# First column tiles in two halves of tokens, and the end of a hybrid encoder layer by column halves and tile by tile

## The chip, the cores and the metric

The kernel runs on one core of a Trainium2 chip. The metric is the device time of one execution in microseconds (us), the median of several runs. A core has five engines that run side by side, each through its own list of instructions in a fixed order: TensorE (PE in the profile, with its weight loads shown as PEld), VectorE (DVE), ScalarE (ACT), GpSimd (POOL) and SyncE (SP, which here only issues DMAs). An instruction waits on semaphores, and what stands behind it on its engine waits with it.

## The reference: what is computed

One encoder layer is applied to two batches with the same weights: P (prompt, 512 tokens) and S (sample, 1024 tokens), 1024 features, float32. Cut to what matters:

```python
u = group_rmsnorm(h, norm_mix_pre); proj = u @ w_in
# z, xbc, dt -> forward and backward chunked state-space scans (SSD head group)
# hy         -> width-3 conv, long convolution with implicit filters (Hyena head group)
mix = concat([y_ssd, y_hy]) @ w_out
h = h + group_rmsnorm(mix, norm_mix_post)
u = group_rmsnorm(h, norm_ffn_pre)
ff = (silu(u @ w_gate) * (u @ w_up)) @ w_down
h = h + group_rmsnorm(ff, norm_ffn_post)
gate = sigmoid(group_rmsnorm(h, ple_norm_pre) @ w_ple_gate)
e = p_l @ w_ple_proj
h = h + group_rmsnorm(gate * e, ple_norm_post)      # the last step of the layer
```

`group_rmsnorm(x, w)` is x divided by the root of the mean of its squares over the 1024 features, times the row `w`.

## The kernel before: tiling, stages and order

**Products.** A float32 operand is split into two `fp32r` parts, hi (a copy on ACT, lines 292 and 325) and lo (the rest, by a subtraction on POOL, line 293, for weights, and on DVE, line 326, for activations). `mm3` (lines 296 to 303) makes one product of three matmuls: hi by hi (L301), hi by lo (L302 or L303), lo by hi. Weights come by DMA into `wst` and are split into `whi` and `wlo`; each of the three has six buffers.

**Stages.** P: the input norm and its transposes (`make_u`, `norm_tile`, lines 328 to 370) give `uh` and `ul`, 1024 features by 512 tokens. `project` (line 431) then makes twelve tiles of 128 columns of `w_in`: `win_T` (line 375) multiplies eight feature blocks into one PSUM tile `g` of 512 tokens, 24 matmuls, and `conv` (line 384) reads it back on ACT and DVE. `gps` has two PSUM tiles, so the third column tile waits until the first has been read by `conv`. The weights of the first three tiles are loaded and split ahead (`pre`, line 1408). Then follow the filters of the long convolution (`filters`, lines 810 to 940), the scans, the long convolution, the same for S, the output projections, and the FFN of P. In the last stretch, for S, `down_group` makes the two groups of 512 tokens ready, and for each group `ple` (line 1374) and `ple_post` (line 1392) do the last two lines of the reference.

**The last group.** `ple` loads `e` into four tiles `ga` (128 tokens by 1024 columns) and calls `tok_gemm` (line 1007) with the gate weights. `tok_gemm` goes over two halves of 512 columns (`nch`), loads the eight feature blocks ("rows" below) of weights in four pairs, and multiplies each pair with four token tiles in the order 0, 2, 1, 3. With `last` set, it holds back the last two pairs of the second half (rows 4 to 7) and runs those tile by tile, so that tile 0 is complete first; 12 matmuls of each tile are then behind one another. After each half, `ev_gate` (line 1383) takes the sigmoid on ACT (L1386) and multiplies it into `ga` on DVE (L1387). `ple_post` calls `post_steps` (line 1040): the sum of squares of a whole row on ACT (L316), `rstd` (L308 on DVE, L309 on POOL), the gain row (L1056), the scaling and the residual (L1057) on DVE, and a DMA of 128 by 1024 to the output, issued by SP (L1061).

**What sets the order.** The program is written stage by stage, but the order of each engine's list is chosen when the program is built: line 1523 asks for a scheduler with a time line of its own estimates, and sections marked as urgent (`high_priority`) go first. So filters, scans and long convolutions are woven between the projection tiles, and a change near the start can alter the weave behind it.

Of the kernel before, what the change touches and what calls it, by code (L numbers as in the profile page):

```python
# [15 lines left out]
ALU = mybir.AluOpType  # L16
# [150 lines left out]
class Kern:  # L167
# [144 lines left out]
    def sumsq(self, pool, x):  # L312

        ss = self.T(self.sp, [128, 1], "ss")
        junk = self.T(pool, [128, x.shape[-1]], "junk", BF16, bufs=1)
        self.nc.scalar.activation(junk, x, AF.Square, accum_out=ss)  # L316
        return ss
# [57 lines left out]
    def win_T(self, q, u, c0, w=128, pre=None):  # L375
# [3 lines left out]
        for g in range(q.ng):  # L379
            for k in range(8):  # L380
                self.mm3(ps[:w, g, :], ws[k], u[g].row(k), k == 0, k == 7)
# [625 lines left out]
    def tok_gemm(self, lhs, nk, wsrc, krow0, evac, last=False, mid=None):  # L1007

        for nch in range(2):
# [7 lines left out]
            for k0 in range(0, nk, 2):  # L1017
# [5 lines left out]
                if last and nch == 1 and k0 + 4 >= nk:  # L1023
# [16 lines left out]
    def post_steps(self, pool, acc, row, res, t0, dst, gain=None, u=None, tags=("t4",) * 4, last=False):  # L1040
# [7 lines left out]
        def load(t):  # L1048
            rts[t] = self.T(pool, [128, 1024], tags[t])
            nc.sync.dma_start(rts[t], res[t0 + t * 128:t0 + (t + 1) * 128, :])  # L1050

        def add(t):
            a, r, rt = acc[t], rs[t], rts[t]
            if last:
                w = self.T(pool, [128, 1024], "t4")
                nc.vector.tensor_tensor(out=w, in0=a, in1=rw, op=ALU.mult)  # L1056
                nc.vector.scalar_tensor_tensor(rt, w, r, rt, ALU.mult, ALU.add)  # L1057
            else:
                nc.vector.scalar_tensor_tensor(a, a, r, rw, ALU.mult, ALU.mult)
                nc.vector.tensor_tensor(out=rt, in0=a, in1=rt, op=ALU.add)  # L1060
            (nc.sync if last else nc.gpsimd).dma_start(dst[t0 + t * 128:t0 + (t + 1) * 128, :], rt)  # L1061
# [38 lines left out]
    def outproj(self, q, g, pool, acc, k0, mix, u=None):  # L1100
# [11 lines left out]
        self.tok_gemm(mix.tok, nk, self.I["w_out"][0], k0 * 128, evac, last)  # L1112
# [9 lines left out]
    def down(self, pool, acc, hidden, m0, cnt):  # L1122
# [3 lines left out]
        def evac(nch, t, ps):  # L1126
# [3 lines left out]
            else:  # L1130
# [3 lines left out]
                      self.I["w_down"][0], m0 * 128, evac, m0 + cnt == NF)  # L1134
# [239 lines left out]
    def ple(self, q, g, pool, u):  # L1374
# [7 lines left out]

        def ev_gate(nch, t, ps):
# [3 lines left out]
            nc.vector.tensor_tensor(out=a, in0=a, in1=sg, op=ALU.mult)  # L1387

        self.tok_gemm(u.tok, 8, I["w_ple_gate"][0], 0, ev_gate, True, load)
        return ga  # L1390

    def ple_post(self, q, g, pool, ga):
        last = q is self.S and g == 1
        self.post(pool, ga, "ple_norm_post", q.h2, g * 512, q.out, last=last,
                  tags=("bh", "bl", "bl", "bh") if last else ("t4",) * 4)

    def build(self):
# [43 lines left out]
        with self.pool("mix_s", side="right") as mp, ExitStack() as right:  # L1441
# [24 lines left out]
            with self.pool("blocks") as tb:  # L1466
# [21 lines left out]
                with self.pool("end_s", side="right") as tr:  # L1488
# [6 lines left out]
                    for g, v in ((0, v0), (1, v1)):  # L1495
                        self.ple_post(S, g, pe, self.ple(S, g, pe, v))
# [30 lines left out]
```

## Time and profile before

| What | us |
|---|---|
| median of 3 runs (2858.03 to 2859.99) | 2858.76 |
| time of the profiled execution | 2855.3 |
| its span, first to last instruction | 2853.5 |
| PE busy | 2691.4 (94%) |
| DVE busy | 1751.1 (61%) |
| ACT busy | 1328.7 (47%) |
| POOL busy | 1389.5 (49%) |

Rows of the time line read: start in us from the span's start, duration in us, engine, line, operation, output tile and input tiles, shape, count; in brackets the idle time of the engine before it and who ended it. `128x512` is 128 partitions by 512 elements. SPq and ACTq rows are DMA issues. Matmuls are pipelined: their shown duration is longer than the distance of their starts, and the distance is what counts. Rows of the stretches ("windows") read: stretch, length, then busy time and number of instructions of PE, PEld, DVE, ACT and POOL, granted clock, DMA share and GB/s. The names of tiles in the listings of order carry a running number.

### The profile page before, as it was taken

Reading aid. Unit: us, or ns where it says so; the run is one execution under the profiler, and the core shown is the slowest. Engines: PE = TensorE matmul, PEld = TensorE weight load, DVE = VectorE, ACT = ScalarE, POOL = GpSimd, SP = SyncE. Lnnn points to the kernel's source line nnn. Section 1 sums busy time; section 2 is a strip of 40 time slices with the busy share of each in tenths; the row PEclk is TensorE's granted clock in tenths of the full one; section 3 lists DMA queues with packets and bytes.
Section 4 is the critical chain, followed back from the end, with each engine's and each line's share of the span. In section 5 each row is a group of like instructions: output and inputs, shape, how many; then the busy total and the mean of one; then the engine's idle time right before and its main releaser. Section 6 shows DMA issues by size and latency. Waiting matters only on the chain.

```text
span 2853.5 us, 41647 instructions
## 1 busy us (share of the span) xinstructions
PE 2691.4 (94%) x14696; PEld 2264.9 (79%) x14696; DVE 1751.1 (61%) x2893; ACT 1328.7 (47%) x2564; POOL 1389.5 (49%) x1137
## 2 busy tenths in 40 slices
PE   7999999999999989889999999987799999999998
PEld 5987888778888767578778777765799999877776
DVE  6767996977666896966676744475444444325345
ACT  4434445773234565745444354465433333345453
POOL 4445555443453555535444444554544444445464
PEclk9999999999999999989999999998899999999999
DMA  5545555744345476778888876565332222366664
GB/s 169 179 137 129 148 174 186 219 140 138 100 121 161 154 247 203 220 209 205 198 182 207 189 220 217 178 230 172 97 97 82 80 73 86 123 207 212 196 205 179
DMA packets 446203, 475.85 MB, mean 167 GB/s; under 512 B 29153, under 2 KB 330025, under 8 KB 443691
## 3 DMA queue, kind: packets, MB, share of 16 engines
q1 hardware_dynamic: 340923, 347.34, 39.7%
q0 software_dynamic: 25920, 63.97, 10.0%
q10 hardware_dynamic: 79152, 61.88, 6.8%
q8 instruction: 116, 1.90, 0.3%
q14 instruction: 92, 0.75, 0.1%
HBM read 346.54 MB, written 91.95 MB: 154 GB/s over the span
## 4 chain that ended last, share of the span: by engine, by line
PE 71%; DVE 14%; DMA 6%; issue 4%; POOL 2%; ACT 2%; SPq 1%; DVEq 0%; POOLq 0%; ACTq 0%
PE g L301 18%; PE g L303 17%; PE g L302 17%; PE a L301 3%; PE a L302 3%; PE a L303 3%; PE a L700 2%; DVE E L615 1%; PE a L973 1%; DVE b L692 1%; PE a L628 1%; PE a L404 1%; DVE W L619 1%; DVE ml L326 1%; POOL wlo L293 1%
## 5 line engine op out<-in xcount | busy, mean ns | idle before, releaser
L293 POOL TENSOR_TENSOR wlo<-wst,whi 128x512 fp32r<-128x512 f32 (+1 forms) x556 | 802.7, 1450 | 762.4 <-ACT whi L292 680.3
L292 ACT ACTIVATE whi<-wst 128x512 fp32r<-128x512 f32 (+1 forms) x556 | 346.9, 629 | 551.5 <-PE g L302 340.8
L301 PE MATMUL g<-uh,whi 128*128 128x512 f32 (+1 forms) x1232 | 493.6, 401 | 8.9 <-DVE cv L393 4.7
L303 PE MATMUL g<-uh,wlo 128*128 128x512 f32 (+1 forms) x1232 | 491.8, 399 | 0.0
L302 PE MATMUL g<-ul,whi 128*128 128x512 f32 (+1 forms) x1232 | 491.1, 399 | 0.0
L301 PE MATMUL g<-bh,whi 128*128 128x256 f32 x1056 | 294.9, 285 | 16.8 <-DVE gt L1227 6.8
L302 PE MATMUL g<-bl,whi 128*128 128x256 f32 x1056 | 296.2, 282 | 0.0
L303 PE MATMUL g<-bh,wlo 128*128 128x256 f32 x1056 | 295.1, 282 | 0.9 <-POOL wlo L293 0.8
L301 PEld LDWEIGHTS g<-uh,whi 128*128 128x128 f32 x1232 | 233.4, 189 | 68.5 <-issue 9.8
L303 PEld LDWEIGHTS g<-uh,wlo 128*128 128x128 f32 x1232 | 232.7, 189 | 53.9 <-issue 5.8
L302 PEld LDWEIGHTS g<-ul,whi 128*128 128x128 f32 x1232 | 232.9, 189 | 53.3 <-issue 6.9
L326 DVE TENSOR_TENSOR ml<-mx,mh 128x512 fp32r<-128x512 f32 x152 | 123.6, 816 | 218.2 <-ACT mh L325 216.9
L393 DVE SCALAR_TENSOR_TENSOR cv<-g,cols,cv 128x510 f32<-128x510 f32 (+3 forms) x192 | 192.9, 1006 | 63.4 <-ACT cv L387 61.3
L285 POOL DMA_DIRECT2D wlo<-wst x132 | 115.6, 932 | 212.4 <-ACT wlo L284 205.4
L301 PEld LDWEIGHTS g<-bh,whi 128*128 128x128 f32 x1056 | 199.3, 191 | 21.7 <-DVE gt L1227 9.0
L303 PEld LDWEIGHTS g<-bh,wlo 128*128 128x128 f32 x1056 | 201.2, 191 | 1.4 <-POOL wlo L293 1.4
L302 PEld LDWEIGHTS g<-bl,whi 128*128 128x128 f32 x1056 | 201.8, 191 | 0.1
L302 PE MATMUL g<-wlo,uh 128*128 128x264 f32 (+1 forms) x576 | 191.4, 332 | 0.5 <-POOL wlo L293 0.5
L303 PE MATMUL g<-whi,ul 128*128 128x264 f32 (+1 forms) x576 | 190.2, 331 | 1.3 <-DVE rs_t L308 1.3
L309 POOL TENSOR_TENSOR rs_t<-rs_t,nhalf 128x1 f32<-128x1 f32 (+2 forms) x112 | 119.9, 1073 | 144.4 <-DVE rs_t L308 143.8
L301 PE MATMUL g<-whi,mh 128*128 128x512 f32 x412 | 171.1, 415 | 19.8 <-ACT mh L325 13.4
L301 PE MATMUL g<-whi,uh 128*128 128x264 f32 (+1 forms) x576 | 189.4, 331 | 0.1
(328 smaller groups left out, 6027.2 us busy)
## 6 DMA issues: line engine op xcount, KB each, us to landing
wst<-in_w_in SPq DMA_DIRECT2D x192, 256.0 KB
wlo<-wst POOLq DMA_DIRECT2D x132, 256.0 KB, 4.9
wst<-in_w_down SPq DMA_DIRECT2D x132, 256.0 KB
wst<-in_w_out SPq DMA_DIRECT2D x96, 256.0 KB
wst<-in_w_gate SPq DMA_DIRECT2D x92, 256.0 KB
wst<-in_w_up SPq DMA_DIRECT2D x92, 256.0 KB
mx<-hid_s SPq DMA_DIRECT2D x88, 256.0 KB
rw<-rows_s SPq DMA_DIRECT2D x32, 512.0 KB
```

What stands on the lines that cost most here:

```text
L285: nc.gpsimd.dma_start(lo, w, accum_op=ALU.add)
L292: nc.scalar.activation(hi, w, AF.Copy)
L293: (eng or nc.gpsimd).tensor_tensor(out=lo, in0=w, in1=hi.bitcast(F32), op=ALU.subtract)
L301: nc.tensor.matmul(ps, lh, rh, start=first, stop=False, skip_group_check=shared)
L302: nc.tensor.matmul(ps, lh, rl, start=False, stop=False, skip_group_check=shared)
L303: nc.tensor.matmul(ps, ll, rh, start=False, stop=last, skip_group_check=shared)
L309: nc.gpsimd.tensor_tensor(out=t[:, :w], in0=t[:, :w], in1=self.nhalf[:, :w], op=ALU.pow)
L326: self.nc.vector.tensor_tensor(out=lo, in0=ps, in1=hi.bitcast(F32), op=ALU.subtract)
L393: nc.vector.scalar_tensor_tensor(out[:, a:b], ps[:, a + d:b + d], wcol(w), out[:, a:b], ALU.mult, ALU.add)
L404: nc.tensor.transpose(ps[:, j * 128:(j + 1) * 128], srcs[i + j], self.ident)
L615: nc.vector.scalar_tensor_tensor(E[:, h], rw[:, 0, h], dbf[:, c, gh:gh + 1], rw[:, 1, h], ALU.add, ALU.min)
L700: nc.tensor.matmul(ps[:, r, c], fw[:, r0 + r, c], sig[:, r0 + r], start=True, stop=True)
```

## The change

Three edits.

1. `win_T`: a tile whose weights were loaded ahead (`pre`, the first three column tiles of P) is made in two halves of 256 tokens, each with its 24 matmuls, instead of one of 512 tokens. The scheduler places everything anew after that.
2. `tok_gemm`: `last` becomes the number of weight pairs that the second half holds back. All earlier callers give 2 as before; the last group gives 3, so rows 2 to 7 run tile by tile, 18 matmuls a tile.
3. The last group of `ple` does the norm and the residual itself: each half's sum of squares (into `hss`) and the product with the gain row follow the half's gate at once; after the second half the two sums are added, `rstd` is taken, and scaling, residual and output go by halves of 512 columns, the first half's DMA from SP, the second's from ACT. `h2` is loaded after the first half into two `t4` and two `bl` buffers. `post_steps` loses its `last` case.

```diff
     def win_T(self, q, u, c0, w=128, pre=None):
...
         for g in range(q.ng):
-            for k in range(8):
-                self.mm3(ps[:w, g, :], ws[k], u[g].row(k), k == 0, k == 7)
+            for c in (slice(0, 256), slice(256, 512)) if pre else (slice(0, 512),):
+                for k in range(8):
+                    self.mm3(ps[:w, g, c], ws[k], [x[:, c] for x in u[g].row(k)], k == 0, k == 7)
...
-                if last and nch == 1 and k0 + 4 >= nk:
+                if last and nch == 1 and k0 + last * 2 >= nk:
...
-            if last:
-                w = self.T(pool, [128, 1024], "t4")
-                nc.vector.tensor_tensor(out=w, in0=a, in1=rw, op=ALU.mult)
-                nc.vector.scalar_tensor_tensor(rt, w, r, rt, ALU.mult, ALU.add)
-            else:
-                nc.vector.scalar_tensor_tensor(a, a, r, rw, ALU.mult, ALU.mult)
-                nc.vector.tensor_tensor(out=rt, in0=a, in1=rt, op=ALU.add)
-            (nc.sync if last else nc.gpsimd).dma_start(dst[t0 + t * 128:t0 + (t + 1) * 128, :], rt)
+            nc.vector.scalar_tensor_tensor(a, a, r, rw, ALU.mult, ALU.mult)
+            nc.vector.tensor_tensor(out=rt, in0=a, in1=rt, op=ALU.add)
+            nc.gpsimd.dma_start(dst[t0 + t * 128:t0 + (t + 1) * 128, :], rt)
...
+        end = q is self.S and g == 1
+        hs = self.T(self.sp, [128, 2, 4], "hss", bufs=1) if end else None
+        res = {}
+
         def ev_gate(nch, t, ps):
             a = ga[t][:, nch * 512:(nch + 1) * 512]
             sg = self.T(pool, [128, 512], "mst")
             nc.scalar.activation(sg, ps, AF.Sigmoid)
             nc.vector.tensor_tensor(out=a, in0=a, in1=sg, op=ALU.mult)
-
-        self.tok_gemm(u.tok, 8, I["w_ple_gate"][0], 0, ev_gate, True, load)
+            if not end:
+                return
+            self.sumsq(pool, a, hs[:, nch, t:t + 1])
+            nc.vector.tensor_tensor(out=a, in0=a, in1=rw[:, nch * 512:(nch + 1) * 512], op=ALU.mult)
+            if nch == 0:
+                res[t] = self.T(pool, [128, 1024], "t4" if t < 2 else "bl")
+                nc.sync.dma_start(res[t], q.h2[g * 512 + t * 128:g * 512 + (t + 1) * 128, :])
+                return
+            ss = hs[:, 0, t:t + 1]
+            nc.vector.tensor_tensor(out=ss, in0=ss, in1=hs[:, 1, t:t + 1], op=ALU.add)
+            r = self.rstd(ss, D)
+            for i, eng in enumerate((nc.sync, nc.scalar)):
+                cs = slice(i * 512, (i + 1) * 512)
+                nc.vector.scalar_tensor_tensor(res[t][:, cs], ga[t][:, cs], r, res[t][:, cs], ALU.mult, ALU.add)
+                eng.dma_start(q.out[g * 512 + t * 128:g * 512 + (t + 1) * 128, cs], res[t][:, cs])
+
+        if end:
+            rw = self.gain_row(pool, "row", "ple_norm_post")
+        self.tok_gemm(u.tok, 8, I["w_ple_gate"][0], 0, ev_gate, 3 if end else 2, load)
         return ga
```

On PE, at the very start of the program, stand before: the transposes of the fourth token tile (into `g_198`), one matmul of the first column tile `g_259`, a product of the filter stage (L843), and the rest of the tile.

```order
L339 MATMUL g_198<-ident_105,cv_153 128x128 x8
L301 MATMUL g_259<-uh_125,whi_211 128x512
L843 MATMUL a_863<-zt_f_844,w_149_846 64x512
L302 MATMUL g_259<-ul_126,whi_211 128x512
L303 MATMUL g_259<-uh_125,wlo_212 128x512
```

And in the changed program (line numbers there are a few higher, and running numbers behind the first three tiles 72 higher):

```order
L339 MATMUL g_198<-ident_105,cv_153 128x128 x8
L301 MATMUL g_259<-uh_125,whi_211 128x256
L302 MATMUL g_259<-ul_126,whi_211 128x256
...
L301 MATMUL g_259<-uh_125,whi_211 128x256
L844 MATMUL a_935<-zt_f_916,w_149_918 64x512
L302 MATMUL g_259<-ul_126,whi_211 128x256
```

The filter product now stands behind the first half's 24 matmuls and the first matmul of the second half.

Further on, still on PE, a step of the filter stage (L906 and L907, output `a_978`) stands before directly behind the projection tile `g_587`:

```order
L302 MATMUL g_587<-ul_126,whi_583 128x512
L303 MATMUL g_587<-uh_125,wlo_584 128x512
L906 MATMUL a_978<-xm_973,kf_919 128x128
L907 MATMUL a_978<-sg_928,kf_919 128x128
L301 MATMUL a_1002<-w4h_911,Hh_902 128x256
```

The same step, now with the name `a_1050`, stands in the changed program behind `g_763`, which was `g_691` before:

```order
L302 MATMUL g_763<-ul_126,whi_759 128x512
L303 MATMUL g_763<-uh_125,wlo_760 128x512
L907 MATMUL a_1050<-xm_1045,kf_991 128x128
L908 MATMUL a_1050<-sg_1000,kf_991 128x128
L301 MATMUL a_1074<-w4h_983,Hh_974 128x256
```

That is two projection tiles, 48 matmuls, later. Up to the long convolution of S, the woven work (filters, scans, long convolutions) stands 0 to 100 matmuls of the main stream later than before; at the end of the scans of S the distance is 0 again, and behind it the two orders are the same but for the last group.

On DVE, the last rows of the program before (`bh_26968` and `bh_26970` are `ga` of tiles 1 and 3, `mst` the sigmoid, `row` the gain):

```order
L1387 TENSOR_TENSOR bh_26968<-bh_26968,mst_27287 128x512
L1057 SCALAR_TENSOR_TENSOR bl_27297<-t_5320_27327,rs_t_27308,bl_27297 128x1024
L1056 TENSOR_TENSOR t_5322_27333<-bh_26968,row_27293 128x1024
L308 TENSOR_SCALAR rs_t_27314<-ss_27311 128x1
L1387 TENSOR_TENSOR bh_26970<-bh_26970,mst_27290 128x512
L1057 SCALAR_TENSOR_TENSOR bl_27331<-t_5322_27333,rs_t_27314,bl_27331 128x1024
L1056 TENSOR_TENSOR t_5324_27339<-bh_26970,row_27293 128x1024
L308 TENSOR_SCALAR rs_t_27320<-ss_27317 128x1
L1057 SCALAR_TENSOR_TENSOR bh_27337<-t_5324_27339,rs_t_27320,bh_27337 128x1024
```

And in the changed program (`bh_27040` and `bh_27042` are tiles 1 and 3):

```order
L1401 SCALAR_TENSOR_TENSOR t_5272_27202<-bh_27039,rs_t_27383,t_5272_27202 128x512 x2
L1401 SCALAR_TENSOR_TENSOR bl_27210<-bh_27041,rs_t_27397,bl_27210 128x512 x2
L1387 TENSOR_TENSOR bh_27040<-bh_27040,mst_27404 128x512
L1391 TENSOR_TENSOR bh_27040<-bh_27040,row_27044 128x512
L1397 TENSOR_TENSOR hss_27043<-hss_27043 128x1
L1387 TENSOR_TENSOR bh_27042<-bh_27042,mst_27418 128x512
L308 TENSOR_SCALAR rs_t_27411<-hss_27043 128x1
L1401 SCALAR_TENSOR_TENSOR t_5278_27218<-bh_27040,rs_t_27411,t_5278_27218 128x512 x2
L1391 TENSOR_TENSOR bh_27042<-bh_27042,row_27044 128x512
L1397 TENSOR_TENSOR hss_27043<-hss_27043 128x1
L308 TENSOR_SCALAR rs_t_27425<-hss_27043 128x1
L1401 SCALAR_TENSOR_TENSOR bl_27226<-bh_27042,rs_t_27425,bl_27226 128x512 x2
```

The gain product is half as wide and stands ahead of the scale; the last tile's gate (L1387) stands ahead of tile 1's scale, and tile 1's two residual halves stand between the last tile's gate and its gain product.

More of the change, by code (lines that the diff above doesn't have):

```diff
@@ L310, in rstd, with sumsq @@
         return t[:, :w]
-    def sumsq(self, pool, x):
-        ss = self.T(self.sp, [128, 1], "ss")
+    def sumsq(self, pool, x, ss=None):
+        ss = self.T(self.sp, [128, 1], "ss") if ss is None else ss
         junk = self.T(pool, [128, x.shape[-1]], "junk", BF16, bufs=1)
@@ L1038, in post, with post_steps @@
             pass
-    def post_steps(self, pool, acc, row, res, t0, dst, gain=None, u=None, tags=("t4",) * 4, last=False):
+    def post_steps(self, pool, acc, row, res, t0, dst, gain=None, u=None):
         nc = self.nc
@@ L1048, in load @@
         def load(t):
-            rts[t] = self.T(pool, [128, 1024], tags[t])
+            rts[t] = self.T(pool, [128, 1024], "t4")
             nc.sync.dma_start(rts[t], res[t0 + t * 128:t0 + (t + 1) * 128, :])
@@ L1111, in outproj @@
         last = k0 + nk == 16
-        self.tok_gemm(mix.tok, nk, self.I["w_out"][0], k0 * 128, evac, last)
+        self.tok_gemm(mix.tok, nk, self.I["w_out"][0], k0 * 128, evac, 2 * last)
         if last:
@@ L1133, in down @@
         self.tok_gemm(lambda k, t: [x[:, t * 128:(t + 1) * 128] for x in hidden[m0 + k]], cnt,
-                      self.I["w_down"][0], m0 * 128, evac, m0 + cnt == NF)
+                      self.I["w_down"][0], m0 * 128, evac, 2 * (m0 + cnt == NF))
     def ffn(self, q, g, pool, u):
@@ L1387, in ev_gate @@
             nc.vector.tensor_tensor(out=a, in0=a, in1=sg, op=ALU.mult)
-        self.tok_gemm(u.tok, 8, I["w_ple_gate"][0], 0, ev_gate, True, load)
+            if not end:
[16 more added lines that the diff above has]
+        self.tok_gemm(u.tok, 8, I["w_ple_gate"][0], 0, ev_gate, 3 if end else 2, load)
         return ga
     def ple_post(self, q, g, pool, ga):
-        last = q is self.S and g == 1
-        self.post(pool, ga, "ple_norm_post", q.h2, g * 512, q.out, last=last,
-                  tags=("bh", "bl", "bl", "bh") if last else ("t4",) * 4)
+        self.post(pool, ga, "ple_norm_post", q.h2, g * 512, q.out)
     def build(self):
@@ L1494, in build @@
                     self.rush(chain)
-                    for g, v in ((0, v0), (1, v1)):
-                        self.ple_post(S, g, pe, self.ple(S, g, pe, v))
+                    self.ple_post(S, 0, pe, self.ple(S, 0, pe, v0))
+                    self.ple(S, 1, pe, v1)
 _INS = ["x_prompt", "x_sample", "p_prompt", "p_sample", "norm_mix_pre", "w_in", "ssd_conv_w", "ssd_conv_b",
```

## The prediction, made before the result

> **What bounds the kernel now.** I read the page first: the busy shares and the chain that ended last.
>
> ```profile
> PE 2691.4 (94%) x14696; PEld 2264.9 (79%) x14696; DVE 1751.1 (61%) x2893; ACT 1328.7 (47%) x2564; POOL 1389.5 (49%) x1137
> PE 71%; DVE 14%; DMA 6%; issue 4%; POOL 2%; ACT 2%; SPq 1%; DVEq 0%; POOLq 0%; ACTq 0%
> ```
>
> TensorE is busy for 94% of the span and makes 71% of the chain. So a gain can come only from the some 160 us in which PE has nothing, and what is gained at one place is kept as long as PE is the bound behind it. The stretches of 50 us show where that holds (PE's busy time is the second number):
>
> ```profile
> 50.00:100.00 50.00, 50.00 (x242) 40.64 (x242) 38.77 (x77) 23.81 (x46) 22.60 (x27) 1.00 0.53 151
> 1000.00:1050.00 50.00, 42.59 (x179) 31.11 (x178) 47.85 (x92) 28.86 (x79) 25.04 (x17) 0.88 0.72 234
> 1150.00:1200.00 50.00, 40.78 (x171) 29.56 (x171) 46.44 (x87) 35.84 (x92) 29.37 (x27) 0.92 0.69 204
> 1200.00:1250.00 50.00, 38.19 (x212) 31.59 (x212) 26.96 (x50) 27.28 (x65) 19.45 (x21) 0.81 0.71 227
> ```
>
> Right behind the head PE is full. At the end of the scans of S it idles for 7.4, 9.2 and 11.8 us of three stretches, 28.4 us in all. The change works at two places where PE waits or is done, the head and the end, and reorders what lies between.
>
> **The head.** The time line at the start, PE, ACT and DVE:
>
> ```profile
> 20.58 1.94 PE L339 MATMUL g<-ident,cv 128*128 128x128 f32 x8 [2.83 <-DVE cv L333]
> 22.56 1.02 ACT L325 ACTIVATE uh<-g 128x1024 fp32r<-128x1024 f32 x1 [3.80 <-PE g L339]
> 23.61 1.23 DVE L326 TENSOR_TENSOR ul<-g,uh 128x1024 fp32r<-128x1024 f32 x1 [1.71 <-ACT uh L325]
> 23.63 0.79 PE L301 MATMUL g<-uh,whi 128*128 128x512 f32 x1 [1.11 <-ACT uh L325]
> 26.34 1.94 PE L843 MATMUL a<-zt_f,w 33*64 33x512 f32 x2 [1.91 <-DMA w<-in_hy_f_w]
> 28.21 0.79 PE L302 MATMUL g<-ul,whi 128*128 128x512 f32 x1
> 30.93 0.57 PE L302 MATMUL g<-ul,whi 128*128 128x512 f32 x1
> 31.34 0.40 PE L303 MATMUL g<-uh,wlo 128*128 128x512 f32 x1
> 34.12 0.40 PE L303 MATMUL g<-uh,wlo 128*128 128x512 f32 x1
> 35.05 0.40 PE L301 MATMUL g<-uh,whi 128*128 128x512 f32 x1
> ```
>
> The first column tile waits for the fourth token tile's hi part, and its second matmul stands behind the filter product, which waits for a DMA until 26.34. From 28.21 the stream runs, 3.1 us at 0.41 a matmul (30.93 to 31.34), then at 0.232 (four matmuls from 34.12 to 35.05). The row at 35.05 begins the second tile. For half tiles the trace has a stream of 256 columns further on, ten matmuls apart:
>
> ```profile
> 2299.88 0.28 PE L303 MATMUL g<-bh,wlo 128*128 128x256 f32 x1
> 2301.07 0.28 PE L301 MATMUL g<-bh,whi 128*128 128x256 f32 x1
> ```
>
> That is 0.119 each. Two halves take 0.238 for 0.232, so 72 added matmuls cost 72 x 0.006 = 0.4 us. The Trainium skill, page "TensorE: Matmul & The Clock Gate", section "Back-to-back issue gap", gives N/2.4 + 2.5 ns a matmul once warm; by that the price would be 72 x 2.5 ns, an estimate of 0.2 us. I keep the rows' 0.4.
>
> The first half needs only tokens 0 to 255, split long before, so it starts when the last transposes end, 20.58 + 1.94 = 22.52. Slow for 3.1 us at 0.205 (15 matmuls), then nine at 0.119: done at 26.7. By then the fourth tile's lo part (23.61 + 1.23) and the filter's DMA (26.34) are there, so neither wait comes back. The filter product takes 1.1 (its row at 40.72, below), 23 halves 2.7: the tile ends at 30.6 instead of 35.05, 4.4 us earlier.
>
> What is late next is PSUM: the third column tile needs the first one's bank, read by `conv` on DVE, where the filter's chain stands ahead of and between the conv steps.
>
> ```profile
> 30.68 0.80 DVE L846 TENSOR_SCALAR ft<-a,vb 64x512 f32<-64x512 f32 x1 [5.84 <-DMA vb<-in_hy_f_freq]
> 31.51 0.42 DVE L847 TENSOR_SCALAR fk<-ft 64x512 f32<-64x512 f32 x1
> 32.42 3.13 DVE L850 SCALAR_TENSOR_TENSOR ft<-fk,ft 64x512 f32<-64x512 f32 x3
> 35.59 0.42 DVE L851 TENSOR_SCALAR ft<-ft 64x512 f32<-64x512 f32 x1
> 36.40 3.10 DVE L393 SCALAR_TENSOR_TENSOR cv<-g,cols,cv 128x510 f32<-128x510 f32 x4 [0.39 <-ACT cv L387]
> 40.72 1.07 PE L843 MATMUL a<-fh,w 64*64 64x512 f32 x2
> 41.71 0.50 PE L301 MATMUL g<-uh,whi 128*128 128x512 f32 x1
> 49.52 0.47 PE L301 MATMUL g<-uh,whi 128*128 128x512 f32 x1 [1.52 <-DVE cv L393]
> ```
>
> That chain waits for a DMA of its own and starts at 30.68 again: 0.80 + 2 x 0.42 + 3.13 + 0.42 + 3.10 = 8.3, so the bank is free at 39.0. The second tile ends at 30.6 + 24 x 0.238 = 36.3. So a new wait of 2.7 us comes in, and the third tile starts at 39.0 instead of 41.71. It and four transposes take 6.1; the fourth starts at 45.1 instead of 49.52, since the old wait of 1.52 has no cause there. That is 4.4 us, of which 1.1 is the second filter product, now behind that point. **The head gives 3.3 us**; 1.6 if nothing but the third tile's earlier start is kept (41.71 - 39.0 = 2.7, less 1.1), 4.4 if the new wait fades.
>
> **The end.** The last tile's rows, and the start of its last transfer:
>
> ```profile
> 2840.66 0.40 PE L303 MATMUL g<-whi,bl 128*128 128x512 f32 x1
> 2841.09 0.60 ACT L1386 ACTIVATE mst<-g 128x512 f32<-128x512 f32 x1
> 2842.69 0.15 DVE L308 TENSOR_SCALAR rs_t<-ss 128x1 f32<-128x1 f32 x1
> 2842.75 0.68 DVE L1387 TENSOR_TENSOR bh<-bh,mst 128x512 f32<-128x512 f32 x1
> 2842.91 0.92 POOL L309 TENSOR_TENSOR rs_t<-rs_t,nhalf 128x1 f32<-128x1 f32 x1 [2.60 <-DVE rs_t L308]
> 2844.43 0.19 ACT L316 ACTIVATION_READ_ACCUMULATOR junk<-bh 128x1 f32 x1
> 2845.07 1.22 DVE L1056 TENSOR_TENSOR t<-bh,row 128x1024 f32<-128x1024 f32 x1
> 2846.43 0.54 POOL L309 TENSOR_TENSOR rs_t<-rs_t,nhalf 128x1 f32<-128x1 f32 x1 [2.60 <-DVE rs_t L308]
> 2847.01 1.29 DVE L1057 SCALAR_TENSOR_TENSOR bh<-t,rs_t,bh 128x1024 f32<-128x1024 f32 x1 [0.66 <-POOL rs_t L309]
> 2848.32 0.33 SPq L1061 DMA_DIRECT2D out<-bh  x1
> 2849.50:2850.00 0.50, 0.00 (x0) 0.00 (x0) 0.00 (x0) 0.00 (x0) 0.00 (x0) 0.50 0.98 401
> ```
>
> PE ends at 2841.06, and DVE, working through four tiles in a row, at 2848.30. The matmuls' end stays where it is. With 18 matmuls a tile, tile 1 is complete at 2841.06 - 18 x 0.232 = 2836.9, earlier than now, but DVE has the list shown in the listing of order. Halves of 512 cost about half of L1057's 1.29, 0.67; the gain product 0.68 as L1387. Tiles 0 and 2 (complete 4.2 us apart) keep DVE until about 2839.7. Tile 1: gate 0.68, square on ACT 0.6 + 0.19, gain 0.68, sum 0.15: 2842.0. Then, in order: last gate 0.68, L308 0.15, POOL's power 0.54 to 0.92, tile 1's two halves 1.34 (2844.7 to 2845.1), last gain 0.68, sum and L308 0.30, power 0.54, two halves 1.34, and 0.2 for hand-overs between engines: 2847.8 to 2848.2, against 2848.30. So the shorter steps nearly all go into the queue: 0.1 to 0.5 us. The power takes 0.92 beside the L1387 of 2842.75 and 0.54 alone. The Trainium skill, page "GPSIMD Engine Reference", section "8. Key points", says that GpSimd shares its SBUF interfaces with VectorE and contends with DVE instructions of two SBUF inputs; by that tile 1's power, in which DVE waits for it, would take the shorter time, and the sum 0.5. The last transfer, 512 KB at 401 GB/s for 1.3 us, becomes 256 KB for 0.65. The ACT queue's DMA issue stands behind the last square, done 4 us earlier; SP's four DMAs have nothing behind them. **The end gives 0.9 us**, from 0 (every power at 0.92, no hand-over hidden) to 2.8 (tile 1's halves out of the way: the last tile's own chain of 5.1 us would end at 2846.2, and the transfer's 0.65).
>
> Three pairs held back fill all six weight buffers, so rows 6 and 7 are split only when pair 0 is through, 72 matmuls before the end, at 2824.4.
>
> ```profile
> 2824.51 2.56 POOL L293 TENSOR_TENSOR wlo<-wst,whi 128x512 fp32r<-128x512 f32 x2 [2.28 <-ACT whi L292]
> 2808.02 7.45 SPq L277 DMA_DIRECT2D wst<-in_w_ple_gate  x4
> ```
>
> POOL finishes them at 2827.1, where it does now; row 7's is needed at 2824.4 + 15 x 0.232 = 2827.9. Slack 0.8 us, cost nothing; one slower split would cost some tenths. The residual loads stand on SP between and behind the last weight loads (issued by 2815.5), 20 us ahead of their use: nothing.
>
> **The weave.** Between 50 and 1250 us the same work runs in another order, filters and scans mostly 20 to 95 matmuls later. No row prices that. I take 0, with about a fifth of the 28.4 us of waits above either way.
>
> **Sum.** 3.3 + 0.9 = 4.2 us off the profiled execution's 2855.3 (span 2853.5), 2851.1; the median shown stands 3.5 above that execution, so 2858.76 - 4.2 = 2854.6.
>
> **The rivals.** 0.2% is 5.7 us, about what a measurement of this kernel can tell from no change: faster is below 2853.0, slower above 2864.5.
>
> - *The lead is eaten at the scans of S.* There DVE is the busier engine (47.85 and 46.44 of 50), and if its chain does not start earlier, PE's lead becomes waiting. Only the end's 0.9 is left: 2857.9. Against it: DVE's work hangs on the same projections. Chance 0.18.
> - *The weave saves too.* The woven steps have more finished work ahead of them, and ACT's list has four table loads fewer; a fifth of the 28.4 us goes as well: 2854.6 - 5.7 = 2848.9. Chance 0.27.
> - *Slower: the lag of the scans is given back where nothing covers it.* Near the end of S's projections the scans stand up to 46 matmuls later, and at their end 0; the last steps have so much less beside them. If DVE cannot catch up, PE waits for it: 46 x 0.232 = 10.7, so 2865.3. It decides once DVE is full behind 1050 us; the order's equal tail and PE's fullness between these stretches speak against it. Chance 0.08.
> - *The halves stall on weight loads.* If a load could not run beside the matmul before it, each of the 72 added ones would cost its load, and the head lose all. The page named first, in "The mechanism", has loads overlap only when the row group differs, which would be this; a load there is an estimate of 0.107 us. The stream above, 0.119 apart with one load each, speaks against it. By rows, with the mean load of 0.19 in view: 72 x 0.19 = 13.7 less the 4.2, so 2868.3. Chance 0.02.
>
> ```profile
> L303 PEld LDWEIGHTS g<-bh,wlo 128*128 128x128 f32 x1056 | 201.2, 191 | 1.4 <-POOL wlo L293 1.4
> ```
>
> **The numbers.** The forecast has 0.45; its own range is 2852 to 2857, and 0.08 of it lies below 2853.0. Faster is 0.27 + 0.08 = 0.35, slower 0.08 + 0.02 = 0.10, the same 0.55. The range 2848.5 to 2861 leaves out the two slow cases and a part of the saving weave, 0.17 together.
>
> **What would show it.** Right: the first L301 near 22.5, the filter product without its 1.9 us wait, the second tile near 30.6, a new wait of some 2.7 us on `conv` before the third, the fourth near 45.1; DVE's last row nearly as far behind PE's end as now, and a last transfer half as long. Wrong: half products further apart than 0.12; PE idle in the three stretches changed by more than 6 us; PE waiting for a low part in the last 17 us.

## The result: slower by half a per cent

The changed kernel takes 2875.78 us (median of 6 runs, 2869.39 to 2879.12) against 2857.49 for the kernel before (6 runs, 2854.19 to 2859.99): ratio 1.0052, 95% interval 1.004 to 1.0064. It is slower by 14.9 us by the ratio and 18.3 by the medians, outside the range. The profiled execution took 2879.12 us, its span is 2877.3.

The head and the end came as forecast; the loss lies in two things between them. The page of the changed kernel, busy shares and chain:

```profile
PE 2700.3 (94%) x14768; PEld 2271.7 (79%) x14768; DVE 1752.9 (61%) x2905; ACT 1323.8 (46%) x2568; POOL 1385.7 (48%) x1137
PE 67%; DVE 15%; DMA 8%; issue 4%; ACT 3%; POOL 3%; SPq 0%; ACTq 0%; DVEq 0%; POOLq 0%
```

PE's share of the chain fell by 4 points and the DMAs' rose by 2: waits have come in. The stretches of 50 us of the changed kernel, and behind them the last stretch of the kernel before:

```profile
50.00:100.00 50.00, 50.00 (x236) 39.58 (x235) 37.17 (x72) 24.13 (x44) 23.64 (x27) 1.00 0.50 138
1000.00:1050.00 50.00, 44.22 (x176) 32.14 (x175) 47.82 (x90) 30.30 (x81) 25.73 (x18) 0.77 0.65 211
1150.00:1200.00 50.00, 41.25 (x172) 29.40 (x171) 46.52 (x92) 34.69 (x90) 30.75 (x29) 0.94 0.66 203
1200.00:1250.00 50.00, 38.95 (x213) 30.60 (x212) 36.34 (x68) 30.26 (x80) 22.47 (x21) 0.85 0.68 197
1250.00:1300.00 50.00, 42.69 (x224) 36.54 (x223) 20.73 (x43) 21.79 (x37) 15.57 (x14) 0.93 0.90 232
```

```profile
1250.00:1300.00 50.00, 48.56 (x254) 40.81 (x253) 37.93 (x70) 25.73 (x47) 21.92 (x19) 1.00 0.93 217
```

In the three stretches that the prediction watched, PE idles for 25.6 us instead of 28.4, so the sign of being wrong that it named there (a change of more than 6 us) does not show. Right behind them, at 1250, it works for 42.7 us instead of 48.6. Stretches at fixed times mislead where one kernel lags, so I matched the instructions: the k-th matmul with the same tiles and shape in both traces is the same work. **The lag** is its start in one kernel less its start in the profiled execution of the kernel before. Below is PE's main stream (all matmuls into `g`), as the median over the 50 us behind the named time of the kernel before; in the last column the lag of the scans of S behind 1225 us, where they end (matched on PE, DVE, ACT and POOL over 25 us).

| kernel | 100 | 1150 | 1500 | 1750 | 2100 | 2450 | scans' end |
|---|---|---|---|---|---|---|---|
| changed kernel | -4.0 | 2.8 | 14.1 | 16.4 | 20.5 | 25.2 | 11 |
| b_head | -4.9 | -3.5 | 5.8 | 7.0 | 11.4 | 11.4 | 5 |
| a_pad64 | -3.8 | 1.1 | 9.3 | 8.3 | 13.3 | 13.4 | 9 |
| b_end32 | -0.4 | 2.8 | 3.9 | 3.6 | 6.8 | 11.9 | 3 |
| b_end64 | -0.5 | -1.3 | -1.4 | -0.5 | 2.6 | 3.8 | -2 |
| shift32 | -0.3 | 0.8 | 1.3 | 4.9 | 7.7 | 12.8 | 1 |
| h_loads | -5.0 | -2.0 | 5.1 | 6.2 | 7.6 | 7.8 | 6 |
| h_loads_end0 | -4.4 | 1.2 | 4.3 | 4.4 | 4.2 | 4.3 | 9 |
| h_nolo | -4.2 | -1.8 | 8.3 | 8.7 | 10.9 | 11.7 | 10 |
| h_mlp_end0 | -4.7 | 4.8 | 5.1 | -3.0 | 1.2 | 1.2 | 4 |
| old_loads | -0.4 | -1.8 | -0.9 | -8.9 | -4.4 | -4.5 | -2 |
| old_late | 0.2 | 1.4 | 7.5 | 12.4 | 18.6 | 19.5 | 1 |

The changed kernel leads by 4 us at 100 us, loses 6.8 up to 1150, 11 between 1150 and 1500, and 4.7 more between 2100 and 2450, where its order is the same, row for row, as before. (From 1750 to 2100 sixteen of the nineteen kernels lose 3 to 8 us against this one execution of the kernel before, so much of that step is probably its own.)

Two things have to be kept in mind. It was said above that behind the scans of S the two orders are the same; on PE they are not. Counted in the traces, the first product of the long convolution of S stands 30 matmuls of the main stream later than before, others up to 51 later, and only from 1450 us on is the distance 0. And where woven work stands later, the main stream alone looks too far ahead. With all of PE's matmuls counted, each by its columns, b_head leads by 4.6 us at 1050, by 0.1 at 1150, and lags by 5.8 at 1500; the changed kernel lags by 2.4, 5.6 and 14.0.

**The first loss.** The start of the changed kernel on PE:

```profile
20.64 1.94 PE L339 MATMUL g<-ident,cv 128*128 128x128 f32 x8 [3.78 <-DVE cv L333]
22.23 0.56 PE L301 MATMUL g<-uh,whi 128*128 128x256 f32 x1
...
26.37 1.04 PE L844 MATMUL a<-zt_f,w 33*64 33x512 f32 x2 [0.31 <-PE g L301]
...
30.17 0.28 PE L301 MATMUL g<-uh,whi 128*128 128x256 f32 x1
...
35.73 0.28 PE L303 MATMUL g<-uh,wlo 128*128 128x256 f32 x1
39.19 0.35 PE L301 MATMUL g<-uh,whi 128*128 128x256 f32 x1 [3.17 <-DVE cv L394]
...
46.91 0.39 PE L301 MATMUL g<-uh,whi 128*128 128x512 f32 x1
...
53.02 1.07 PE L844 MATMUL a<-fh,w 64*64 64x512 f32 x2
```

The tiles start where they were forecast. The filter's second product, the last row, starts at 53.02 instead of 40.72: 12.3 us later. With it goes everything that hangs on the filters: the scans, the long convolution, the scans of S. Far on, the first product of the scans of S of one kind, in the kernel before and in the changed one:

```profile
905.95 0.38 PE L607 MATMUL a<-lct,lbt 128*128 128x128 f32 x2
```

```profile
917.09 0.38 PE L608 MATMUL a<-lct,lbt 128*128 128x128 f32 x2
```

The lag is still there, 11.1 us. Where the scans of S end, the kernel before has this on ACT, SP and PE (the scans' last store, the loads of the long convolution of S, its first matmul):

```profile
1237.18 0.37 ACTq L661 DMA_DIRECT2D mix_s<-mt  x1
1239.64 0.33 SPq L949 DMA_DIRECT2D fw<-cst_fwd_s  x1
1240.50 0.43 SPq L953 DMA_DIRECT2D b<-g_s  x1
1243.99 0.92 POOL L285 DMA_DIRECT2D wlo<-wst  x1 [13.53 <-ACT wlo L284]
1251.31 2.84 PE L700 MATMUL a<-b,fw 128*128 128x128 f32 x24
```

And the changed kernel:

```profile
1247.33 0.92 POOL L285 DMA_DIRECT2D wlo<-wst  x1 [7.45 <-ACT wlo L284]
1248.09 0.37 ACTq L662 DMA_DIRECT2D mix_s<-mt  x1
1251.63 0.48 SPq L950 DMA_DIRECT2D fw<-cst_fwd_s  x1
1252.69 0.43 SPq L954 DMA_DIRECT2D b<-g_s  x1
1269.14 4.69 PE L701 MATMUL a<-b,fw 128*128 128x128 f32 x24 [7.31 <-DMA b<-g_s]
```

The scans' last store comes 10.9 us later and the loads behind it 12, now after the first copies of low parts by DMA (POOL's L285) and no longer ahead of them. PE waits 7.31 us for `b`; before, it did not wait for these 24 matmuls, with 30 matmuls fewer ahead of them.

**The second loss** is a steady one. 300 us of the FFN of S, where PE is full, in the kernel before and, 21 us later, in the changed kernel:

```profile
2150.00:2450.00 300.00, 298.27 (x2519) 296.06 (x2518) 126.09 (x136) 103.78 (x179) 145.28 (x106) 1.00 0.27 82
```

```profile
2171.00:2471.00 300.00, 298.29 (x2486) 296.04 (x2484) 122.73 (x136) 102.05 (x176) 143.69 (x104) 1.00 0.27 80
```

Same order, same clock (1.00), 33 matmuls fewer: 120.7 ns a matmul for 119.1. Edit 3 allocates the small tile `hss`, 32 bytes a partition, ahead of the large buffers, so `uh`, `ul`, `bh`, `bl` and others start 32 bytes later.

**The end**, DVE, POOL and ACT from PE's last matmul on:

```profile
2865.43 0.40 PE L303 MATMUL g<-whi,bl 128*128 128x512 f32 x1
2866.49 0.69 DVE L1387 TENSOR_TENSOR bh<-bh,mst 128x512 f32<-128x512 f32 x1 [0.46 <-ACT mst L1386]
2867.33 0.54 POOL L309 TENSOR_TENSOR rs_t<-rs_t,nhalf 128x1 f32<-128x1 f32 x1 [5.71 <-DVE rs_t L308]
2867.90 1.41 DVE L1401 SCALAR_TENSOR_TENSOR t<-bh,rs_t,t 128x512 f32<-128x512 f32 x2 [0.65 <-POOL rs_t L309]
2870.25 0.54 POOL L309 TENSOR_TENSOR rs_t<-rs_t,nhalf 128x1 f32<-128x1 f32 x1 [2.39 <-DVE rs_t L308]
2870.83 1.42 DVE L1401 SCALAR_TENSOR_TENSOR bl<-bh,rs_t,bl 128x512 f32<-128x512 f32 x2 [0.66 <-POOL rs_t L309]
2872.28 0.34 ACTq L1402 DMA_DIRECT2D out<-bl  x1
```

DVE ends 6.42 us behind PE (2865.43 + 0.40 to 2872.25) instead of 7.24 (2841.06 to 2848.30), and the span 11.5 instead of 12.5.

### The profile page after: what moved, and what is told of

It is laid out like the page before. It is cut to its first block, busy times and chain, and to the rows that moved or that the text cites. A ratio compares the mean times of both kernels' runs of the same rounds, so it can differ in the third digit from the quotient of the medians.

```text
span 2877.3 us, 41811 instructions
## 1 busy us (share of the span) xinstructions
PE 2700.3 (94%) x14768; PEld 2271.7 (79%) x14768; DVE 1752.9 (61%) x2905; ACT 1323.8 (46%) x2568; POOL 1385.7 (48%) x1137
## 4 chain that ended last, share of the span: by engine, by line
PE 67%; DVE 15%; DMA 8%; issue 4%; ACT 3%; POOL 3%; SPq 0%; ACTq 0%; DVEq 0%; POOLq 0%
PE g L301 17%; PE g L303 17%; PE g L302 16%; PE a L303 3%; PE a L301 3%; PE a L302 3%; PE a L701 2%; DVE E L616 1%; DMA mx<-mix_s 1%; PE a L974 1%; DVE W L620 1%; PE a L405 1%; POOL rs_t L309 1%; DVE b L693 1%; POOL wlo L293 1%
## 5 line engine op out<-in xcount | busy, mean ns | idle before, releaser
L293 POOL TENSOR_TENSOR wlo<-wst,whi 128x512 fp32r<-128x512 f32 (+1 forms) x556 | 800.5, 1446 | 789.2 <-ACT whi L292 749.9
L301 PEld LDWEIGHTS g<-uh,whi 128*128 128x128 f32 x1256 | 237.6, 189 | 69.2 <-issue 11.7
L285 POOL DMA_DIRECT2D wlo<-wst x132 | 115.4, 938 | 224.5 <-ACT wlo L284 220.6
L301 PEld LDWEIGHTS g<-bh,whi 128*128 128x128 f32 x1056 | 199.7, 191 | 25.2 <-DVE gt L1223 8.1
```

Of the source, the lines that this page charges most:

```text
L285: nc.gpsimd.dma_start(lo, w, accum_op=ALU.add)
L293: (eng or nc.gpsimd).tensor_tensor(out=lo, in0=w, in1=hi.bitcast(F32), op=ALU.subtract)
L301: nc.tensor.matmul(ps, lh, rh, start=first, stop=False, skip_group_check=shared)
```

## The experiments

Every median is given with its ratio to the kernel before, measured beside it (its medians there: 2856.64 to 2858.23), and the 95% interval. Single runs of one kernel lie 7 to 18 us apart, so a profiled execution is one draw, and small differences need the medians.

### The parts alone

**b_head**, edit 1 alone:

```diff
+            for c in (slice(0, 256), slice(256, 512)) if pre else (slice(0, 512),):
+                for k in range(8):
+                    self.mm3(ps[:w, g, c], ws[k], [x[:, c] for x in u[g].row(k)], k == 0, k == 7)
```

> The kernel before with edit 1 alone (the first three column tiles in two halves), so with the changed kernel's order up to the last group and no hss, that is no shift of buffers. Theory A (the new order costs some 13 us net of the head's gain, the shift 6, the end gives 1): 2875.8 - 6 + 1 = 2871, with PE waiting about 7 us for the DMA of b<-g_s at the start of the long convolution of S, and 117 ns between products of bh and bl. Rival (the loss is in the new end or in the shift, the order costs nothing): 2857.5 - 3 = 2854.5, and no such wait.

2866.07 us, 1.0033 (1.002 to 1.0047). Edit 1 loses 9.4 us by itself. The filter's second product and PE's wait are as in the changed kernel; the loads are 6 us later than before, not 12:

```profile
52.19 1.07 PE L844 MATMUL a<-fh,w 64*64 64x512 f32 x2
...
1242.35 0.37 ACTq L662 DMA_DIRECT2D mix_s<-mt  x1
1245.90 0.33 SPq L950 DMA_DIRECT2D fw<-cst_fwd_s  x1
1263.22 5.33 PE L701 MATMUL a<-b,fw 128*128 128x128 f32 x24 [7.18 <-DMA b<-g_s]
```

**b_end32**, edits 2 and 3 alone, `hss` as in the change:

> The changed kernel with the first column tiles whole again, so with the order of the kernel before up to the last group, and hss of 32 bytes. Theory A: 2857.5 + 6 for the shift - 1 for the end = 2862.5, with 118 to 119 ns between products of bh and bl. Rival (only the order costs): 2856.5.

2869.05, 1.0036 (1.0024 to 1.0049): 12 us slower without any new order, more than forecast.

**b_end64**, the same with `hss` of 64 bytes:

```diff
-        hs = self.T(self.sp, [128, 2, 4], "hss", bufs=1) if end else None
+        hs = self.T(self.sp, [128, 4, 4], "hss", bufs=1) if end else None
```

> As the run with the end alone and 32 bytes, with hss of 64 bytes. Theory A: the end's 1 us alone is left, 2856.5, and 117 ns between products of bh and bl. Rival (the shift is nothing): the same time as with 32 bytes.

2859.64, 1.0008 (0.9996 to 1.0021). Of the 12 us the 32 bytes more give back 9, though the 117 ns did not come (see a_pad64).

**a_pad64**, the changed kernel with that line:

> The changed kernel, but the new tile hss takes 64 bytes a partition instead of 32, so that the buffers allocated behind it (uh, ul, bh, bl and others) start 64 bytes later than before the change, not 32. Same order on every engine as the changed kernel. Theory A (a shift by 32 bytes slows the matmuls that read these buffers): the 256-wide products of bh and bl are 117 ns apart again instead of 118 to 119, 3136 of them give some 6 us back: 2870. Rival (the wider spacing is of the run or the chip, or of the order): spacing stays at 118 to 119 and the time at 2876.

2866.94, 1.0029 (1.002 to 1.0038): what is left is b_head's loss. Its stretch is full again:

```profile
2163.00:2463.00 300.00, 298.29 (x2519) 295.75 (x2519) 133.95 (x136) 103.45 (x179) 144.50 (x105) 1.00 0.27 81
```

But it is full as a sum of two opposite differences. The products of `bh` and `bl` into `g` are 117.6 to 118.1 ns apart in this stretch (kernel before 117.0 and less, changed kernel 118.2 to 119.3), so the expected 117 did not come back; those into `a` are 113.3 to 113.4 apart, before 119.2 to 119.5. b_end64 is alike.

**shift32**, nothing of the change, only an unused tile:

```diff
+        nc.gpsimd.memset(self.T(self.sp, [128, 8], "pad", bufs=1), 0.0)
```

> The kernel before with one unused tile of 32 bytes a partition (one memset on POOL) ahead of the buffers, nothing else: every operation and its order as before, uh, ul, bh, bl and what stands behind them 32 bytes later. Theory A (the shift alone costs 8 to 9 us, as between the two ends): 2865, with 118 to 119 ns between products of bh and bl and 234 to 235 between products of uh with whi. Rival (the shift costs only together with the new end, or the two earlier comparisons were chance): 2857.

2867.26, 1.0031 (1.0019 to 1.0042): 9.2 us for 32 bytes. The same stretch:

```profile
2159.00:2459.00 300.00, 298.28 (x2484) 295.82 (x2483) 123.98 (x136) 102.37 (x177) 142.69 (x104) 1.00 0.27 80
```

Theory A is shown in its main point: the shift by 32 bytes costs by itself, in the old order and the new and with either end. Which start address gives which distance is not settled by these runs. By ratios it is 9 us alone, 8 with the end (1.0036 less 1.0008) and 7 in the changed kernel (1.0052 less 1.0029).

### Halves with other orders

**h12**, only the first two tiles in halves (`if pre and c0 < 2304`):

> The kernel before with the first two column tiles in halves and the third whole. PE's order is then the old one from the filters to the scans of S; only in the long convolution of S some work stands up to 57 matmuls earlier. Theory B (the halves give their 3 us, the order at the end of the scans of S takes 9 to 13): 2854, PE waiting at most 2 us for b<-g_s, and a lag that stays at -2 to -4 us up to 1200 us. Rival (the halves themselves bring PE out of step, whatever the order): about 2866 as with edit 1 alone.

2862.79, 1.0011 (1.0 to 1.0022), between the two. The scans of S end only 3.5 us late, but the lead of 3.5 us is lost between 100 and 250 us. I had expected the lead to stay; it doesn't.

**h12_end0**, the same with the new end and `hss` in a buffer that is there already:

```diff
+        hs = self.T(self.pools["x"][1], [128, 16], "hss")[:, :8].rearrange("p (a b) -> p a b", a=2)
```

> The first two column tiles in halves and the new end, with hss in an existing buffer of the same name, so that no buffer is shifted. If the three causes add (order, shift, end): head -3, end -1, nothing else, 2853 and faster than before and after. Rival (the end gives nothing, or the halves cost later): 2856 to 2866.

2863.03, 1.0012 (1.0 to 1.0024), the rival's side: like h12.

### Is it the wait for `b`?

**h_loads**, edit 1 with the loads of the long convolution of S in another order:

```diff
             nc.sync.dma_start(fw, self.cst["fwd_" + q.nm])
+            gts = {b: load_g(b) for b in range(2)} if q is self.S else {}
             nc.sync.dma_start(iv, self.cst["inv_" + q.nm])
```

> Edit 1 alone with its order, but at the start of the long convolution of S the second block of b<-g_s (0.5 MB) is issued right behind the first, ahead of iv and K (1 MB each). Theory B (PE's wait of 7.3 us there is the queue in front of that block): the wait falls to 0 to 2 us and the time from 2866 to 2859 to 2861. Rival (the wait only moves to the next load, K or iv, or the loss arises elsewhere in the order): 2864 to 2867.

2855.9, 0.9996 (0.9983 to 1.0008): 10 us gained, so theory B looked right. But the order has moved too: products of the convolution stand up to 27 matmuls earlier than in b_head. Its profiled execution, 6.7 us above that median, still has a wait of 5.9 us for `b`.

**old_loads**, the control, those loads in the kernel before:

> The kernel before with nothing changed but the loads at the start of the long convolution of S: the second block of b<-g_s right behind the first, ahead of iv and K. A control for the run with edit 1 and the same loads, which took 10 us less than edit 1 alone. Theory B (those 10 us are the new order's own loss, given back): nothing to give back here, PE's wait for b<-g_s stays under 2 us, 2857 as before. Rival (that order of loads is simply better, and hides the new order's loss): 2847 to 2850.

2848.47, 0.9971 (0.9958 to 0.9985). The rival's number, so h_loads proves nothing of the new order's loss. Nor are the loads the reason: the lag falls by 8 us between 1500 and 1750, where this kernel's order of the long convolution of S has moved by up to 57 matmuls as well. The stretch in the kernel before and in old_loads:

```profile
1600.00:1650.00 50.00, 43.50 (x211) 35.96 (x210) 33.22 (x58) 18.21 (x29) 20.80 (x15) 0.86 0.78 183
```

```profile
1600.00:1650.00 50.00, 47.52 (x223) 39.08 (x224) 26.50 (x45) 29.25 (x45) 20.62 (x18) 0.97 0.89 222
```

**h_loads_end0**, all three edits, no shift, those loads:

> All three edits, with hss in an existing buffer (no shift) and the two blocks of b<-g_s loaded ahead of iv and K: the best of what the runs point to. If the parts add: edit 1 with those loads 2855.9, end -1, so 2855, 0.1% under the kernel before. Rival (the loads' gain was chance): 2865.

2854.69, 0.9992 (0.9983 to 1.0). PE still waits 5.6 us for `b`, but the lag rises by 3 us between 1150 and 1500 instead of 8 to 11, and not at all from 1750 to 2100.

**old_late**, the kernel before with a load of 1 MB, not used, ahead of the others:

```diff
+            if q is self.S:
+                early = self.T(sp, [128, R, 2, 128], "b8", bufs=self.b8)
+                nc.sync.dma_start(early.rearrange("p r c n -> p (r c n)"), q.K[0])
```

> The kernel before with one load of 1 MB (a block of K_s, not used) issued ahead of fw, iv and b<-g_s at the start of the long convolution of S, so that those come some 4 to 5 us later, in the old order. Theory B (PE has no slack at that place, in the old order it waits already 0.4 to 1.1 us there): PE waits 3 to 5 us for b<-g_s and the time is 2861 to 2863. Rival (other work covers a late start there, so the wait seen in the new order is not what costs): 2857 to 2858.

2866.56, 1.0033 (1.002 to 1.0046), twice what was expected. PE's first matmul there:

```profile
1262.36 5.46 PE L700 MATMUL a<-b,fw 128*128 128x128 f32 x24 [9.97 <-DMA K<-K_s]
```

PE waits there without edit 1 as well, so the old head leaves no slack for a late load. The time is not the load's alone: products of the convolution also stand up to 27 matmuls later than before.

**h_nolo**, edit 1, the first eight low parts of the FFN of P made by POOL and not by DMA (`self.dma_lo = m > 1` in its loop):

> Edit 1 alone with its order, but the first eight weight loads of the FFN of P are split by POOL's subtraction instead of by a DMA into wlo (256 KB each), so that these eight DMAs don't run beside the loads of fw, iv, b<-g_s and K. Theory C (the scans of S end later against PE's stream, so these loads, which waited for the scans' last store, run into the copies into wlo): PE's wait for b<-g_s falls from 7.2 us to under 3, the step of the lag between 1200 and 1500 us from 8 to 3 to 5 us, and the time from 2866 to 2859 to 2863. Rival (the loads come late whatever runs beside them): wait 6 to 7 us, time 2864 to 2868.

2868.14, 1.0039 (1.0025 to 1.0053). The first wait for `b` fell from 7.2 to 1.1 us (4.3 less the 3.2 of a later one), and the time did not follow. PE's waits from 1150 to 1520 us (total, times, longest):

```profile
PE a L657 <- ACT y L650: 8.5, 1, 8.5
PE g L301 <- DVE acc L1132: 6.2, 4, 2.4
PE a L701 <- DMA b<-g_s: 4.3, 2, 3.2
```

The lag rises by 10 us between 1150 and 1500 all the same, over half of it now ahead of 1225. The first row is a wait for the scans: POOL's subtractions (L293) take 19.4 us from 1150 to 1250 instead of b_head's 10.3, and the scans end 10 us late.

**old_nolo**, its control:

> The kernel before with the same eight splits on POOL, as a control. Its order differs from the old one in the long convolution of S behind (up to 57 matmuls earlier, as in the run with the loads moved in the old order, which gave 8 us at 1600 to 1650 us). Theory C: nothing at 1225 to 1300 us (a step of 0 to 2 us as before), so any gain lies at 1600 to 1650 us: 2847 to 2858. Rival (the copies into wlo cost in either order): a gain of 3 us and more between 1200 and 1300 us.

2857.65, 1.0 (0.9987 to 1.0013): 9 us lost from 1150 to 1500, 9 gained from 1500 to 1750, where its order has moved as old_loads' has. So theory C's wait went and its gain did not come: POOL's work took the place of the DMAs'.

### Is it the lag of the filters?

**h_mlp**, edit 1 with the first stage of the filters of P marked as urgent:

```diff
-                        H = self.filt_mlp(q, sp, mp)
+                        with self.tc.high_priority() if q is self.P else ExitStack():
+                            H = self.filt_mlp(q, sp, mp)
```

> Edit 1 alone (all three tiles in halves), with the first stage of the filters of P marked as urgent: the filter's second product (L843 before) stands again behind the second column tile, where the old order has it, and not behind the fourth; from 70 us on PE's order is the old one up to the scans of S, and in the long convolution of S some work stands up to 57 matmuls earlier. Theory D (in the new order that product starts 11.5 us later, at 52.2 instead of 40.7 us, and with it the chain filters, scans, long convolution, scans of S, whose steps are 8 to 11 us late all the way to 1240 us; the scans of S bound PE there, so the lag returns as waiting): the second product starts by 43 us, the scans of S are at most 3 us late, the step of the lag between 1200 and 1500 us falls from 8 to under 3, and the time from 2866 to 2856 to 2859, less where the moved long convolution gains as it did. Rival (the lag of that chain is a companion, the loss is in the halves or at the loads themselves): 2864 to 2868 with a step of 6 to 10 us between 1200 and 1500.

2856.13, 0.9995 (0.9982 to 1.0007), theory D's number. But its profiled execution, 8.7 us above, has a step of 9.9 us from 1150 to 1500.

**old_mlp**, the control:

> The kernel before with the same mark on the filters, as a control: PE's order is unchanged up to the scans of S and shifted by up to 25 matmuls in the long convolution of S. Theory D: nothing to gain, the filter's second product at 40.7 us as before, 2857. Rival (the mark itself helps): 2850 or less.

2863.32, 1.0019 (1.0008 to 1.0031): 5 us slower, by an order that differs by 25 matmuls in the long convolution of S alone. Neither theory had that. The waits of PE show where it begins:

```profile
PE a L700 <- issue: 7.2, 1, 7.2
```

This is the wait of b_head, ahead of the same products, with the old head: the profile names no releaser, but the loads are issued 2.5 us later than before (`fw` at 1242.13 for 1239.64). If these loads are what it waits for, so little is enough.

**h_mlp_end0**, all edits, no shift, the mark:

> All three edits without the shift (hss in an existing buffer), and the first stage of the filters marked as urgent: the run with the mark, whose profiled execution was 9 us above its median, with the new end. Theory D (the chain's lag was the order's price): 2856.1 - 1 = 2855, and in a profiled execution near the median a step of the lag between 1200 and 1500 us of at most 3 us. Rival (the step of 8 us stays with the halves, and the gain of that run came in the long convolution of S behind it, 8 us at 1550 to 1700 us): the same time, but a step of 6 to 9 us followed by a gain of 8.

2855.03, 0.9992 (0.9981 to 1.0003). The filter's second product is back in its place:

```profile
38.21 1.07 PE L845 MATMUL a<-fh,w 64*64 64x512 f32 x2 [1.58 <-ACT fh L856]
```

The step between 1150 and 1500 is gone (4.8 to 5.1), as theory D says. But the lead is lost before, 5 us of it between 150 and 250 and the rest up to 1150, so at 1500 this kernel stands at 5.1, where b_head stands at 5.8. The 10 us by which it beats b_head arise between 1500 and 1750, in the moved long convolution. So the rival is right about where the gain comes from, and theory D only about the step.

**h_mlp_loads_end0**, the same with the loads of h_loads:

> The same with the two blocks of b<-g_s loaded ahead of iv and K as well. If the gain of those loads in the old order (8.5 us, found at 1550 to 1700 us, where this kernel's order has moved in the same way already) is that move and not the loads: 2855, as without. Rival (the loads themselves gain): 2846 to 2848.

2853.94, 0.9986 (0.9976 to 0.9995): the loads add 1 us where the long convolution has moved already. In all eight kernels with that move the lag falls by 7.9 to 9.4 us from 1500 to 1750; in the eleven others, the changed kernel among them, it changes by -1.0 to 4.9. That settles old_loads: its gain is the move and not the loads, so it no longer speaks against theory B. In the new order, where that move is absent, the same loads gave 10 us by the median, but there the convolution's order moved in another way (h_loads).

**old_loads_end0**, what the runs point to: the kernel before with the new end, no shift, and those loads:

> The kernel before with edits 2 and 3 without the shift (hss in an existing buffer) and the two blocks of b<-g_s ahead of iv and K: no halves, the old order up to the long convolution of S. If the end's 1 us adds to the 8.5 us of those loads: 2847.5. Rival (the end gives nothing): 2848.5, which this run can hardly tell from it; the end is read in its trace, from PE's last matmul to the span's end: 11.5 us instead of 12.4.

2848.87, 0.9965 (0.9952 to 0.9977): 0.35% faster than the kernel before and 0.9% than the changed one, without halves. Its end shows 11.5 us.

## Why the prediction was wrong

**The head was right.** First half at 22.23 (forecast 22.5), no wait of 1.91 us before the filter's first product, the second tile at 30.17 (30.6), a new wait of 3.17 us on `conv` (2.7), the third tile at 39.19 (39.0), the fourth at 46.91 (45.1; 46.10 in b_head, where the lead between 50 and 100 us is 3.7 us). Half products are (35.73 - 30.17) / 47 = 0.118 us apart, so weight loads do not stall them and that rival is out.

**The end was right in its sum, not in its terms.** In all nine kernels with the new end the span ends 11.5 us behind PE's last matmul, in nine of the eleven with the old end 12.5 (in h_nolo and old_nolo 11.8): 0.95 us for 0.9. But DVE gave 0.82 of it (forecast 0.1 to 0.5) and the transfer only the rest (0.65). Both powers take 0.54, with DVE waiting for them, where one took 0.92 beside DVE's L1387 before. That agrees with what the Trainium skill, page "GPSIMD Engine Reference", section "8. Key points", says of the shared SBUF interfaces. The held-back pairs cost nothing: the waits view shows no wait of PE in its last 20 us.

**The step that failed** is the weave: "No row prices that. I take 0". Edit 1 costs 9.4 us by itself, its own lead of 3 to 4 us included. What I missed stands in the prediction: "of which 1.1 is the second filter product, now behind that point". I booked that product at its own length. It is the second link of a chain that runs through filters, scans and the long convolution to the scans of S, and it moved by 12 us. In the new order that chain is 5 to 11 us late at its end, and there PE has no slack (old_late and old_mlp have the wait without edit 1). That the move of this one product makes the chain late is argued and not shown: h_mlp puts it back, and with it the rest of the order up to the scans of S. The first rival was right on the lead: it is eaten at the scans of S, where b_head goes from 4.6 us ahead at 1050 to 0.1 at 1150 with all matmuls counted. The rival with 0.08, a lag given back uncovered, had the place and nearly the price (10.7 us; steps of 8 to 11 in the three kernels with the new order and the old loads), though with a DMA as the releaser where I had DVE.

So most of the price is paid at the start of the long convolution of S, where PE waits for loads that come late because the scans end late: 7.18 us in b_head, and a slow start behind it. h_loads takes the price away with another order of the loads, by the medians only, since the profiled executions of h_loads and h_loads_end0 keep waits of 5.9 and 5.6 us. What no run separates from the late loads is the order of the convolution itself: it is up to 51 matmuls later in the changed kernel, and h_loads and old_late moved it too.

**What was not in the sum at all** is where the buffers lie. `hss` is in the diff; I priced its instructions and not its 32 bytes, and they cost as much as the new order: 7 to 9 us. The forecast for b_end32 had it at 6, from the FFN of S alone.

**Open** is whether halves can keep their lead at all. Without the chain's lag the step at 1150 to 1500 us is gone (h_mlp_end0), but that order loses the lead earlier, where PE has new waits of 2.1 and 1.4 us for two tiles of the filters (`EF`, `xm`) from DVE; no run removes them. Open is also the last microseconds of the sum: by the ratios, 0.33% for edit 1 and 0.36% for the end with its shift make 0.69% where 0.52% was measured (0.4 to 0.64), so the parts agree with the whole only within their intervals.

## What to carry to other kernels

Where a scheduler places the work, an edit of a few instructions buys a new order, and orders differ by more than the edits: with the old head 2848 to 2863 us (old_loads, the kernel before, old_mlp), with edit 1 2856 to 2866 (h_loads, h_mlp, b_head). Look which chain an early, short instruction heads, and price the move of that chain, not the instruction. A new tile, however small, moves every buffer allocated behind it: compare start addresses before and after, and keep small additions in existing buffers. An experiment that lets the order move needs a control for the order, and a match of the two traces instruction by instruction shows in which stretch a difference arises, if all of an engine's work is counted and not one stream of it: h_mlp met theory D's number for another reason.

## What the runs showed of the hardware

- **Buffers 32 bytes further on.** Full stretches of the FFN of S hold 2484 to 2486 matmuls in 300 us (b_end32, shift32, the changed kernel) instead of 2513 to 2520 (the others looked at, those shifted by 64 bytes among them): about 1.6 ns on each product of 256 columns, on average, at a clock of 1.00. The shift by 64 bytes is not neutral product by product: those into `g` take up to 1.4 ns more than before, those into `a` 6 less. In the 512-wide products the distance from `uh` by `whi` to the next rises from 231.8 to 233.6 ns (mean over some 1060, gaps left out). The Trainium skill, page "SBUF — State Buffer", section "Operand start alignment", speaks of which starts are legal and says that it timed nothing; these runs give a price.
- **A wait costs more than its length.** Behind the wait of 7.31 us the 24 matmuls at 1269.14 took 4.69 us, before 2.84; behind 7.18 us 5.33, behind 9.97 us 5.46. The granted clock over these matmuls is 0.60, 0.52 and 0.50, before 1.00. The Trainium skill, page "TensorE: Matmul & The Clock Gate", section "HAM oscillation — how this bites in real kernels", has this: a wait of over about 3.4 us lets the clock fall to half. The trace agrees, and the prediction should have added 1.9 to 2.6 us to a wait of this length where it weighed one.
